# One Trainium2 core, a two-block transformer kernel: the first norm's scales by GpSimd's power operation

## The chip, the cores and the metric

The kernel runs on one core of one Trainium2 chip, as one launch. A core has five engines with queues of their own: TensorE (PE; its weight loads are listed apart as PEld), VectorE (DVE), ScalarE (ACT), GpSimd (POOL) and SyncE (SP), which here issues most DMA transfers. The metric is device time in microseconds (us) of the whole execution; the time of a kernel is the median of several runs.

## The reference, cut to what matters

A sequence of 512 rows of width 1024 goes through two transformer blocks in float32. Only the opening of the first block is touched by this change:

```python
h = x * rsqrt(mean(x * x, axis=-1) + 1e-6) * norm_mix      # rmsnorm, x is 512 x 1024
p = h @ w_in                                               # 1024 x 3872
# p feeds a retention mixer (rope from positions, chunks of 128)
# and an RWKV-7 mixer (token shift, decay and gate from low-rank products,
# a recurrence over time); then cross-attention over a memory of 256 rows,
# an MLP, and a second block with attention and a gated spatial mixer.
```

## The kernel before

Everything is held in float32, and a product that has to be exact is made as three reduced products: each operand is split into a high part (`wh`, or the first tile of a pair) and a low part (`wl`), and `mm3` multiplies high by high, high by low and low by high. The weights come as 189 units of 128x1024 in the order of use. For each unit SP issues one DMA into a `raw` buffer, ScalarE makes `wh` by a cast (line 291), and VectorE or GpSimd makes `wl` by a subtraction (line 292); the function is `pump(u, ahead, SC, E)`, and with `E` given that engine does the subtraction. `raw` has three buffers, so unit 3's transfer waits until unit 0 has been split.

`first()` is the opening. The rows of x are loaded as four blocks of 128 rows, `xb[0]` to `xb[3]`, by SP in the order block 0, block 1, the gain row `g` spread over 128 partitions, block 2, block 3, then units 0 and 1, constants, unit 2. Four helpers work on a block b: `square(b)` sums its squares on ScalarE; `chain(i)` makes the reciprocal roots of a pair of blocks on VectorE, by an integer guess and three Newton steps on 128x2 numbers (13 instructions with the scaling of the mean); `scale(b)` multiplies the block by its root and by the gain, in two halves of 512 columns; `turn(b)` transposes the scaled block on TensorE, four 128x128 tiles to a PSUM bank, and splits each bank into high and low, the high part by a cast on ScalarE and the low part by a subtraction on VectorE (`transp`, `psplit`). Blocks 0 and 1 are scaled on VectorE by one instruction that multiplies by root and gain together. For blocks 2 and 3 GpSimd multiplies x by the gain beforehand and ScalarE multiplies by the root.

After the turns, 48 matmuls of 256 columns make the first product `wa` (unit 0), first for rows 0 to 255 and then for rows 256 to 511; the PSUM tile `ps` is returned. Three pumps are in `first()`: unit 0 with its subtraction on GpSimd, unit 1 on VectorE, unit 2 on GpSimd.

`V`, `SC` and `G` in `first()` are the three engines wrapped by `Ordered`, which keeps the instructions that go through one wrapper in the order of the program; TensorE's wrapper `T` does so for the whole kernel. All other instructions are put in order, engine by engine, by a planner that simulates the program while it is built. The wrapper `G` is kept as `self.G`: `trig()` issues through it the argument reduction for sine and cosine of the retention's rope, 54 GpSimd instructions, nearly all on 128x128 numbers (the first one is the cast to `posf`), so these come behind all that `first()` puts on GpSimd. The two `Sin` activations (line 687) are on ScalarE. In the trace all that goes through a wrapper carries line 220.

After `first()`, `main()` runs one product after another (`tile_t`, 24 matmuls of 512 columns for a unit) and spawns side work (`lora`, `key`, `value`, `recept`) that uses the same engines between the products; its parts in the trace are lines 1412 to 1492.

Of the kernel before, what the change touches and what calls it, by code (L numbers as in the profile page):

```python
# [12 lines left out]
AF = mybir.ActivationFunctionType  # L13
ALU = mybir.AluOpType
# [4 lines left out]
NB = 4  # L19
D = 1024  # L20
KT = 8
# [207 lines left out]
class Kern:  # L229
# [74 lines left out]
    def mm3(self, ps, a, b, first, last):  # L304
        (ah, al), (bh, bl) = a, b
        mm = self.T.matmul
        mm(ps, ah, bh, start=first, stop=False)
        mm(ps, ah, bl, start=False, stop=False)
        mm(ps, al, bh, start=False, stop=last)
# [128 lines left out]
    def first(self):  # L438

        nc, A = self.nc, self.A  # L440
        self.zb = self.mp.tile([P, 128], mybir.dt.bfloat16, name="zb")
        nc.gpsimd.memset(self.zb, 0.0)
        xa, xc = self.slab(4, [P, 2, 1024]), self.slab(5, [P, 2, 1024])
        xb = [xa[:, 0], xa[:, 1], xc[:, 0], xc[:, 1]]
        ya, yc = self.slab(8, [P, 2, 1024]), self.slab(9, [P, 2, 1024])
        xg = [ya[:, 0], ya[:, 1], yc[:, 0], yc[:, 1]]
        ident = self.cp.tile([P, P], F32, name="ident")
        nc.scalar.dma_start(ident, A["cst"][:, 0:P])
        self.ident = ident
        load = lambda b: nc.sync.dma_start(xb[b], A["x"][b * 128:b * 128 + 128])  # L450
        load(0)
        load(1)
        g = self.gain("norm_mix", 6)
        load(2)
        load(3)
        self.prefetch(0)
        self.prefetch(1)
        derived = self.consts()
        self.prefetch(2)
        hh, h1 = self.act4((0, 1, 2, 3))  # L460

        V, SC, G = Ordered(self.tc, nc.vector), Ordered(self.tc, nc.scalar), Ordered(self.tc, nc.gpsimd)
        v = [self.small(2) for _ in range(2)]
        rs = {}
        junk = self.slab(10, [P, 1024])

        def square(b):
            SC.activation(junk, xb[b], AF.Square, accum_out=v[b // 2][:, b % 2:b % 2 + 1])

        def chain(i):  # L470
            V.tensor_scalar(v[i], v[i], 1.0 / D, 1e-6, op0=ALU.mult, op1=ALU.add)
            r = self.rsqrt(v[i], 2, V=V)
            rs[2 * i], rs[2 * i + 1] = r[:, 0:1], r[:, 1:2]

        def scale(b):
            for h in range(2):
                c = slice(h * 512, h * 512 + 512)
                if b < 2:
                    V.scalar_tensor_tensor(xg[b][:, c], xb[b][:, c], rs[b], g[:, c], op0=ALU.mult, op1=ALU.mult)
                else:  # L480
                    SC.activation(xg[b][:, c], xg[b][:, c], AF.Copy, scale=rs[b])

        turn = lambda b: self.transp(xg[b], b, hh, V, SC, ("tp", "ch")[b % 2])
        for b in range(NB):
            square(b)
        for b in (2, 3):
            G.tensor_tensor(xg[b], xb[b], g, op=ALU.mult)
        chain(0)
        scale(0)
        scale(1)  # L490
        chain(1)
        turn(0)
        self.pump(0, 0, SC, G)
        turn(1)
        scale(2)
        scale(3)
        turn(2)
        turn(3)
        h, l = self.spl.pop(0)
        self.u = 1  # L500
        ps = self.psum("mm")
        for off in (0, 256):
            for k in range(KT):
                ah, al = h1[k]
                self.mm3(ps[:, off:off + 256], (h[:, k * 128:k * 128 + 128], l[:, k * 128:k * 128 + 128]),
                         (ah[:, off:off + 256], al[:, off:off + 256]), k == 0, k == KT - 1)
        derived(V)
        self.pump(1, 0, SC, V)
        self.pump(2, 0, SC, G)
        self.G = G  # L510
        return h1, ps
# [1191 lines left out]
```

## Time and profile before

| | us |
|---|---|
| median of 3 runs | 1331.93 |
| lowest and highest of them | 1331.39, 1334.37 |
| the profiled execution, its own time | 1330.39 |
| its span in the trace | 1328.6 |
| TensorE busy in the span | 1257.8 (95%) |
| VectorE, GpSimd, ScalarE busy | 699.8, 536.7, 507.7 |

The span runs from the first to the last instruction of the trace; the profiled execution's own time is 1.79 us more. A view of the trace gives the start of an instruction in us from the start of the span, then its length; in brackets stand the time that its engine sat idle before it and what ended that wait. A line with "x4" holds four instructions, and its length then reaches from the start of the first to the end of the last. TensorE's clock is given as the granted share, where 1.00 is 2.4 GHz and 0.50 is 1.2 GHz.

### The profile page before, as it was taken

Reading aid. Unit: us, or ns where it says so; the run is one execution under the profiler, and the core shown is the slowest. Engines: PE = TensorE matmul, PEld = TensorE weight load, DVE = VectorE, ACT = ScalarE, POOL = GpSimd, SP = SyncE. Lnnn points to the kernel's source line nnn. Section 1 sums busy time; section 2 is a strip of 40 time slices with the busy share of each in tenths; the row PEclk is TensorE's granted clock in tenths of the full one; section 3 lists DMA queues with packets and bytes.
Section 4 is the critical chain, followed back from the end, with each engine's and each line's share of the span. In section 5 each row is a group of like instructions: output and inputs, shape, how many; then the busy total and the mean of one; then the engine's idle time right before and its main releaser. Section 6 shows DMA issues by size and latency. Waiting matters only on the chain.

```text
span 1328.6 us, 18213 instructions
## 1 busy us (share of the span) xinstructions
PE 1257.8 (95%) x6988; PEld 1043.1 (79%) x6988; DVE 699.8 (53%) x1465; ACT 507.7 (38%) x899; POOL 536.7 (40%) x544
## 2 busy tenths in 40 slices
PE   4999799998997989998999999999999999999997
PEld 4667577887895888888888888888887888788886
DVE  5667424456495275546333333332779946665355
ACT  5434323333344234433433322332534435554332
POOL 4924545135666553246311111110214563222474
PEclk9989899899999999999999999999999999999999
DMA  5223313211234422313333233333332232122321
GB/s 188 76 62 83 76 53 72 74 56 41 80 113 143 141 64 80 95 49 111 111 95 96 95 95 96 96 100 100 101 114 80 80 111 64 48 64 64 111 80 64
DMA packets 52376, 117.06 MB, mean 88 GB/s; under 512 B 23072, under 2 KB 23712, under 8 KB 52288
## 3 DMA queue, kind: packets, MB, share of 16 engines
q1 hardware_dynamic: 52112, 115.82, 28.6%
q8 instruction: 55, 0.90, 0.3%
q14 instruction: 33, 0.27, 0.1%
q0 software_dynamic: 32, 0.00, 0.0%
q10 hardware_dynamic: 144, 0.07, 0.0%
HBM read 112.46 MB, written 3.41 MB: 87 GB/s over the span
## 4 chain that ended last, share of the span: by engine, by line
PE 78%; POOL 7%; DVE 7%; issue 3%; ACT 2%; DMA 2%; SPq 0%; DVEq 0%; ACTq 0%; POOLq 0%
PE mm L220 64%; PE ch L220 7%; PE tp L220 4%; POOL s L220 3%; PE cs L220 3%; POOL o L1581 1%; DVE sm L362 1%; POOL s L1583 1%; DVE s L873 1%; DVE sm L358 1%; DMA s<-x 1%; DMA s<-dm 1%; POOL wl L220 0%; ACT t L1056 0%; ACT wh L291 0%
## 5 line engine op out<-in xcount | busy, mean ns | idle before, releaser
L220 PE MATMUL mm<-s,wh 128*128 128x512 f32 (+1 forms) x1424 | 422.5, 378 | 0.0
L220 PE MATMUL mm<-wh,s 128*128 128x512 f32 (+1 forms) x1264 | 364.1, 364 | 7.8 <-DVE s L873 7.8
L220 PEld LDWEIGHTS mm<-s,wh 128*128 128x128 f32 x1424 | 259.1, 191 | 53.2 <-issue 9.7
L220 PEld LDWEIGHTS mm<-wh,s 128*128 128x128 f32 x1264 | 231.2, 192 | 47.2 <-DVE s L873 9.6
L220 PE MATMUL mm<-s,wl 128*128 128x512 f32 (+1 forms) x704 | 263.5, 374 | 0.0
L291 ACT CAST wh<-raw 128x1024 fp32r<-128x1024 f32 x151 | 158.6, 1051 | 250.2 <-PE mm L220 220.2
L292 POOL TENSOR_TENSOR wl<-raw,wh 128x1024 fp32r<-128x1024 f32 x75 | 180.5, 2408 | 156.7 <-ACT wh L291 140.5
L220 PE MATMUL mm<-wl,s 128*128 128x512 f32 (+1 forms) x632 | 227.0, 359 | 2.0 <-POOL wl L292 1.7
L292 DVE TENSOR_TENSOR wl<-raw,wh 128x1024 fp32r<-128x1024 f32 x76 | 95.3, 1253 | 120.9 <-ACT wh L291 120.6
L220 PEld LDWEIGHTS mm<-s,wl 128*128 128x128 f32 x704 | 134.2, 191 | 21.3
L220 PEld LDWEIGHTS mm<-wl,s 128*128 128x128 f32 x632 | 121.9, 193 | 19.1 <-POOL wl L292 2.1
L1074 POOL TENSOR_TENSOR t<-t 128x512 f32<-128x512 f32 x32 | 50.0, 1563 | 214.8 <-ACT t L1073 214.8
L220 PE MATMUL mm<-s,whx 128*128 128x512 f32 (+1 forms) x336 | 100.2, 378 | 0.0
L220 PE MATMUL mm<-whx,s 128*128 128x512 f32 (+1 forms) x272 | 86.5, 377 | 0.6 <-DVE s L873 0.6
L347 DVE TENSOR_TENSOR s<-t,s 128x512 fp32r<-128x512 f32 x44 | 38.6, 877 | 69.9 <-ACT s L346 69.9
L292 POOL TENSOR_TENSOR wlx<-raw,whx 128x1024 fp32r<-128x1024 f32 x18 | 43.7, 2426 | 75.0 <-ACT whx L291 75.0
L220 PEld LDWEIGHTS mm<-s,whx 128*128 128x128 f32 x336 | 62.2, 194 | 10.6 <-DVE s L873 0.4
L220 PE MATMUL ch<-s,s 128*64 128x64 f32 (+3 forms) x504 | 65.2, 274 | 2.5 <-DVE s L873 1.8
L938 DVE TENSOR_TENSOR s<-mm,s 128x256 f32<-128x256 f32 x96 | 35.7, 419 | 58.7 <-PE mm L220 58.5
L291 ACT CAST whx<-raw 128x1024 fp32r<-128x1024 f32 x35 | 36.8, 1052 | 70.6 <-PE mm L220 54.4
L220 PE MATMUL mm<-s,wlx 128*128 128x512 f32 (+1 forms) x168 | 63.2, 376 | 0.0
L220 PEld LDWEIGHTS ch<-s,s 128*64 128x64 f32 (+2 forms) x504 | 47.0, 154 | 16.5 <-DVE s L873 3.7
(268 smaller groups left out, 1703.6 us busy)
## 6 DMA issues: line engine op xcount, KB each, us to landing
raw<-wst SPq DMA_DIRECT2D x189, 512.0 KB, 3.6
s<-x SPq DMA_DIRECT2D x8, 512.0 KB, 5.6
s<-rows SPq DMA_DIRECT2D x7, 512.0 KB, 4.0
out<-t SPq DMA_DIRECT2D x8, 256.0 KB, 2.3
t<-mem SPq DMA_DIRECT2D x2, 512.0 KB, 3.9
dm<-s SPq DMA_DIRECT2D x10, 64.0 KB, 2.0
s<-dm SPq DMA_DIRECT2D x2, 256.0 KB, 4.3
s<-dm SPq DMA_DIRECT2D x8, 64.0 KB, 2.5
```

The lines of the kernel that those rows point to most:

```text
L220: r = getattr(self.eng, name)(*a, **k)
L291: (SC or nc.scalar).copy(h, r)
L292: (E or (nc.gpsimd if self.lowpart(self.nspl) else nc.vector)).tensor_tensor(l, r, h.bitcast(F32), op=ALU.subtract)
L347: self.nc.vector.tensor_tensor(dst[1], src, dst[0].bitcast(F32), op=ALU.subtract)
L358: V.scalar_tensor_tensor(t, y, h, y, op0=ALU.mult, op1=ALU.mult)
L362: V.scalar_tensor_tensor(y, t, 1.5, y, op0=ALU.add, op1=ALU.mult)
L873: (V or self.nc.vector).tensor_tensor(dst[1], ps, dst[0].bitcast(F32), op=ALU.subtract)
L938: self.nc.vector.tensor_tensor(xs, ps[:, c], xs, op=ALU.add)
L1074: nc.gpsimd.tensor_tensor(q, r, r, op=ALU.mult)
L1581: G.tensor_tensor(tv, w[:, 0:k, s:s + 1].broadcast_to([P, k, n]), m[:, s:s + 1, s + 1:32].broadcast_to([P, k, n]), op=ALU.mult)
L1583: G.tensor_tensor(w[:, 0:k, s + 1:32], w[:, 0:k, s + 1:32], tv, op=ALU.add)
```

## The change

The reciprocal roots of the first norm are no longer made by Newton steps on VectorE for pairs of blocks. For each block by itself VectorE adds the epsilon to the mean, and GpSimd raises it to the power -0.5 with one 128x1 instruction, whose exponent comes from a small tile `mh` that GpSimd fills at the start. All four blocks are scaled on VectorE by the instruction that multiplies by root and gain together, so GpSimd's two multiplications by the gain and ScalarE's four multiplications by the root are gone. Unit 0's low part is made on VectorE instead of GpSimd. The order is written anew: `square(3)` comes behind the casts of `turn(0)`, `scale(2)` and `scale(3)` come between the turns, and the product of rows 0 to 255 is cut in two, with k from 0 to 3 issued between `turn(2)` and `turn(3)` and k from 4 to 7 behind `turn(3)`.

```diff
--- before.py
+++ after.py
@@ -460,50 +460,50 @@
         hh, h1 = self.act4((0, 1, 2, 3))
 
         V, SC, G = Ordered(self.tc, nc.vector), Ordered(self.tc, nc.scalar), Ordered(self.tc, nc.gpsimd)
-        v = [self.small(2) for _ in range(2)]
-        rs = {}
+        v = self.small(4)
+        rs, mh = self.small(4), self.small(4)
+        G.memset(mh, -0.5)
         junk = self.slab(10, [P, 1024])
 
         def square(b):
-            SC.activation(junk, xb[b], AF.Square, accum_out=v[b // 2][:, b % 2:b % 2 + 1])
-
-        def chain(i):
-            V.tensor_scalar(v[i], v[i], 1.0 / D, 1e-6, op0=ALU.mult, op1=ALU.add)
-            r = self.rsqrt(v[i], 2, V=V)
-            rs[2 * i], rs[2 * i + 1] = r[:, 0:1], r[:, 1:2]
+            SC.activation(junk, xb[b], AF.Square, accum_out=v[:, b:b + 1])
 
         def scale(b):
+
+            V.tensor_scalar(v[:, b:b + 1], v[:, b:b + 1], 1.0 / D, 1e-6, op0=ALU.mult, op1=ALU.add)
+            G.tensor_tensor(rs[:, b:b + 1], v[:, b:b + 1], mh[:, b:b + 1], op=ALU.pow)
             for h in range(2):
                 c = slice(h * 512, h * 512 + 512)
-                if b < 2:
-                    V.scalar_tensor_tensor(xg[b][:, c], xb[b][:, c], rs[b], g[:, c], op0=ALU.mult, op1=ALU.mult)
-                else:
-                    SC.activation(xg[b][:, c], xg[b][:, c], AF.Copy, scale=rs[b])
+                V.scalar_tensor_tensor(xg[b][:, c], xb[b][:, c], rs[:, b:b + 1], g[:, c], op0=ALU.mult, op1=ALU.mult)
 
         turn = lambda b: self.transp(xg[b], b, hh, V, SC, ("tp", "ch")[b % 2])
-        for b in range(NB):
-            square(b)
-        for b in (2, 3):
-            G.tensor_tensor(xg[b], xb[b], g, op=ALU.mult)
-        chain(0)
-        scale(0)
-        scale(1)
-        chain(1)
-        turn(0)
-        self.pump(0, 0, SC, G)
-        turn(1)
-        scale(2)
-        scale(3)
-        turn(2)
-        turn(3)
-        h, l = self.spl.pop(0)
-        self.u = 1
-        ps = self.psum("mm")
-        for off in (0, 256):
-            for k in range(KT):
+
+        def product(off, ks):
+            h, l = wa
+            for k in ks:
                 ah, al = h1[k]
                 self.mm3(ps[:, off:off + 256], (h[:, k * 128:k * 128 + 128], l[:, k * 128:k * 128 + 128]),
                          (ah[:, off:off + 256], al[:, off:off + 256]), k == 0, k == KT - 1)
+
+        square(0)
+        square(1)
+        square(2)
+        scale(0)
+        scale(1)
+        turn(0)
+        square(3)
+        scale(2)
+        turn(1)
+        self.pump(0, 0, SC, V)
+        wa = self.spl.pop(0)
+        self.u = 1
+        scale(3)
+        turn(2)
+        ps = self.psum("mm")
+        product(0, range(4))
+        turn(3)
+        product(0, range(4, 8))
+        product(256, range(8))
         derived(V)
         self.pump(1, 0, SC, V)
         self.pump(2, 0, SC, G)
```

## Rows read from the trace of the kernel before

**Rows 1.** The page: busy us of the engines; shares of the chain.

```profile
PE 1257.8 (95%) x6988; PEld 1043.1 (79%) x6988; DVE 699.8 (53%) x1465; ACT 507.7 (38%) x899; POOL 536.7 (40%) x544
...
PE 78%; POOL 7%; DVE 7%; issue 3%; ACT 2%; DMA 2%; SPq 0%; DVEq 0%; ACTq 0%; POOLq 0%
```

**Rows 2.** The chain that ended last, 0 to 90: start, us, what.

```profile
28.09 2.50 POOL wl L220
...
72.62 0.31 ACT sin L687
...
76.78 1.77 PE tp L220 x2
```

**Rows 3.** VectorE in order of time, 0 to 42.

```profile
7.25 0.65 DVE L220 TENSOR_SCALAR sm<-sm 128x2 f32<-128x2 f32 x4 [7.25 <-ACT s L220]
...
9.62 6.93 DVE L220 SCALAR_TENSOR_TENSOR s<-s,sm,s 128x512 f32<-128x512 f32 x4
...
10.29 5.60 DVE L220 SCALAR_TENSOR_TENSOR s<-s,sm,s 128x512 f32<-128x512 f32 x2
...
16.47 2.79 DVE L220 TENSOR_SCALAR sm<-sm 128x2 f32<-128x2 f32 x4
...
20.86 1.28 DVE L220 TENSOR_TENSOR s<-tp,s 128x512 fp32r<-128x512 f32 x2
...
27.10 1.23 DVE L220 TENSOR_TENSOR wl<-raw,wh 128x1024 fp32r<-128x1024 f32 x1
```

**Rows 4.** ScalarE in order of time, 0 to 42.

```profile
1.18 1.28 ACT L220 ACT_TABLE_LOAD   x1 [1.18 <-PEq L1696]
...
5.64 0.19 ACT L220 ACTIVATION_READ_ACCUMULATOR s<-s 128x1 f32 x1
...
6.06 1.06 ACT L220 ACTIVATE s<-s 128x1024 f32<-128x1024 f32 x1 [0.23 <-DMA s<-x]
...
9.69 1.06 ACT L220 ACTIVATE s<-s 128x1024 f32<-128x1024 f32 x1 [2.48 <-DMA s<-x]
...
25.53 0.59 ACT L220 CAST s<-ch 128x512 fp32r<-128x512 f32 x1 [0.27 <-PE ch L220]
...
26.01 2.00 ACT L220 CAST wh<-raw 128x1024 fp32r<-128x1024 f32 x2
```

**Rows 5.** GpSimd in order of time, 0 to 42.

```profile
9.76 5.58 POOL L220 TENSOR_TENSOR s<-s,s 128x1024 f32<-128x1024 f32 x2 [6.00 <-DMA s<-x]
...
15.95 2.81 POOL L220 TENSOR_TENSOR wl<-raw,wh 128x1024 fp32r<-128x1024 f32 x1 [0.61 <-ACT wh L220]
...
30.53 0.19 POOL L220 CAST posf<-posi 128x4 f32<-128x4 int32 x1
...
35.26 0.45 POOL L220 TENSOR_TENSOR s<-s 128x128 f32<-128x128 f32 x1
```

**Rows 6.** TensorE in order of time, pieces of 0 to 90.

```profile
21.82 1.97 PE L220 MATMUL tp<-ident,s 128*128 128x128 f32 x8 [3.91 <-ACT s L220]
...
25.15 0.78 PE L220 MATMUL mm<-s,wh 128*128 128x256 f32 x2
...
31.32 0.63 PE L220 MATMUL mm<-s,wh 128*128 128x512 f32 x2
...
76.78 1.77 PE L220 MATMUL tp<-t,cst 2*128 2x512 f32 x2 [2.55 <-ACT t L1448]
...
82.06 1.91 PE L220 MATMUL ch<-ident,t 128*128 128x128 f32 x8
```

**Rows 7.** SP's DMA queue, 0 to 10: the issue that waited for the gain row.

```profile
8.39 0.33 SPq L533 DMA_DIRECT2D s<-lora  x1
```

**Rows 8.** Waits of SP's queue, 0 to 10: us in total, times, longest.

```profile
SPq L533 <- DMA s<-rows: 2.0, 1, 2.0
```

**Rows 9.** Windows: length, busy PE, PEld, DVE, ACT, POOL, granted clock, DMA.

```profile
78.00:80.00 2.00, 2.00 (x5) 1.23 (x5) 1.41 (x3) 0.60 (x2) 0.31 (x2) 0.50 0.00 0
...
82.00:84.00 2.00, 2.00 (x10) 1.94 (x9) 1.29 (x3) 0.58 (x1) 0.00 (x0) 0.51 0.00 0
```

## The prediction

> **What bounds the kernel now.** I read the page first: TensorE is busy for 1257.8 us, 95% of the span, and 78% of the chain that ended last is its own work [rows 1]. So what happens before TensorE's steady run moves the end one for one, unless a second chain stands beside it. I followed the chain of waits through the first 90 us and then each engine in order of time. The chain does not join TensorE at its first product. From 28.09 us it is GpSimd's: unit 2's low part, then the sine reduction without a gap until ScalarE's `Sin` at 72.62, then the `tanh` and copy work queued behind it, and only at 76.78 TensorE, which had waited 2.55 us for it [rows 2, 6]. The reduction cannot begin before unit 2's low part (its first cast, to `posf`, is at 30.53 [rows 5]), and that starts 0.08 us after ScalarE's two casts of units 1 and 2, from 26.01 to 28.01 [rows 4]. These casts follow the last cast of `turn(3)`, which begins at 25.53. So the date that counts is that cast, and the price of the whole change is how much earlier it comes. TensorE's own date beside it is the first matmul of unit 1, at 31.32 [rows 6].
>
> Why is that cast so late? A multiplication of `scale(0)` and `scale(1)` gives way to the next after 0.67 us when nothing is in the way (9.62 to 10.29), but the second and third take 2.8 us each (5.60 for both), next to GpSimd's two multiplications in 5.58 us; the four take 6.93 [rows 3, 5]. The first of the small instructions of `chain(1)` is stretched the same way next to GpSimd's subtraction at 15.95, so that four of them take 2.79 us, and the other nine run to 20.9. Only then ScalarE can scale blocks 2 and 3.
>
> **The change part by part.** *Removed.* GpSimd's two multiplications and its subtraction, 5.58 + 2.81 us, and with them the stretching: four multiplications on VectorE fall from 6.93 to some 2.8 us. Both Newton chains go, 26 small instructions, of which `chain(1)` held VectorE from 16.47 to 20.9 us. ScalarE's four multiplications, which waited for `chain(1)`, go too.
>
> *Added on VectorE's path.* Four more multiplications of 0.67 us = 2.7, unit 0's subtraction 1.23 (as unit 1's at 27.10 [rows 3]), and four round trips to GpSimd. A round trip is the small instruction, 0.16 (four of them in 0.65 [rows 3]), a hand-over of 0.08 each way (as ScalarE to GpSimd above) and the power itself. VectorE is in order, so it stands still meanwhile: `scale(1)` waits behind it, and behind `scale(2)` the subtractions of `turn(1)`. No row shows a power. From below the nearest row is a GpSimd cast of 128x4, 0.19 us; from above a whole pass over 1024 columns, 2.81 us [rows 5]. A power of one number per partition is nearer to the small ones; I take the 0.45 us of a 128x128 product, which is to say that one power costs as much as 128 multiplications. A round trip is then 0.16 + 0.16 + 0.45 = 0.77 us.
>
> The Trainium skill (GPSIMD Reference, 2.1 Instruction dispatch) says that the first call of a freshly loaded kernel pays about 6 us for loading code; no row here shows this, and by it the sum would be an estimated 1332.4 us, 3.8 later.
>
> *The new order, step by step.* `square(0)` ends at 5.83 [rows 4], so the first power is ready at some 6.6. The gain row stands in the way: SP's issue that waited 2.0 us for it goes out at 8.39 [rows 7, 8]. I take 8.4 for the first multiplication, against 9.62 before. VectorE then:
> - `scale(0)`, 2 x 0.67: to 9.76
> - `scale(1)`, 0.77 + 1.34: to 11.87
> - two subtractions of `turn(0)`, pitch 0.6 (two in 1.28 [rows 3]): to 13.07. Their casts come behind `square(2)`, whose block lands at 9.6 and which ends at 10.9 [rows 4]; they end at 12.0, in time.
> - `scale(2)`: to 15.18
> - subtractions of `turn(1)`: to 16.4. ScalarE does `square(3)` from 12.0 to 13.3 and these casts to 14.4, in time; then unit 0's cast to 15.5.
> - unit 0's subtraction: to 17.6
> - `scale(3)`: to 19.7.
>
> TensorE has `turn(2)` done by then, and two of the twelve matmuls of the first part of the product; the third needs unit 0's low part, so ten remain at 17.6. Their price depends on the clock. The 48 matmuls of this product run from 25.15 to 31.32, 0.13 us each, but the first two take 0.78 together. The transposes tell why: eight take 1.97 us at 21.82 and 1.91 at 82.06, inside a window granted 0.51 [rows 6, 9]. So up to some 26 us TensorE is at the lower level, whatever the share printed there, and the clock rose with TensorE at work without a gap since 21.82. I cost the ten at twice 0.13: to 20.2. `scale(3)` ends first, so `turn(3)` starts at 20.2, its eight transposes end at 22.2, and its last cast starts there instead of at 25.53. From that cast to the end of unit 2's cast it was 28.01 - 25.53 = 2.48 us, so it is now at 24.7: 3.3 us earlier.
>
> The remaining 36 matmuls of the product take 0.13 each at the higher level, 4.7 us, or 6.2 if the first twelve are still slow: unit 1 starts at 26.9 to 28.4, earlier by 2.9 to 4.4. Its low part is there by 25 (cast to 23.8, subtraction 1.23). TensorE's date moves about as far as GpSimd's or farther, and TensorE waits later, at 76.78, for GpSimd's branch, so GpSimd's 3.3 us is what the chain gets. GpSimd's four powers lie in a stretch where it now has nothing else, and `mh` is filled at the start. SP's queue is unchanged: raw 3 leaves once unit 0 is split, at 17.6 instead of 18.8. The weight DMAs and everything behind 77 us hang on these dates alone and move along.
>
> Against the profiled execution's own 1330.39 the sum is 1327.1. That execution lies 1.54 below the median of 1331.93, so I forecast **1328.6 us** as a median. A measurement of this kernel tells about 0.2%, 2.7 us, from no change, so this is just beyond it.
>
> **The bounds.** The power enters twice (`scale(1)` and `scale(2)`) as long as the ten matmuls end after `scale(3)`, that is up to 1.55 us; beyond that three times. At 0.19 us the gain is 3.3 + 2 x 0.26 = 3.8. At 2.81 it is 3.3 - 2 x 1.1 - 3 x 1.26 = -2.7, and `scale(0)`'s own power, out at 8.9, adds 0.5: 3.2 us slower. If the ten run at 0.13 they end at 18.9; `turn(3)` then starts behind the first half of `scale(3)`, at 19.1, and ends at 21.1, or, if its transposes are faster too, half of them behind the second half, at some 20.4: 1.1 to 1.8 more gain, 1326.8 to 1327.5.
>
> **The rivals.**
> 1. *Part of the gain is eaten inside the opening.* Either a power of 0.75 to 1.9 us (gain 2.7 down to 0), or a wait of `scale(0)` for `square(2)`, since the four sums are now columns of one tile and `square(2)` comes first in the program: the first multiplication then starts at 10.9 + 0.77 = 11.7 instead of 8.4, and the gain is gone. For such a wait speaks nothing but the order; against it that `square(0)` is through at 5.83 while `square(1)` still waits, to 6.06, for the other half of the same slab to land [rows 4]. Or a first power that loads code: it has 8.4 - 6.1 = 2.3 us of cover, and at the price of ScalarE's table load, 1.28 us [rows 4], it would be hidden; a load of 5.6 us would eat all. Time 1329 to 1332; chance 0.27.
> 2. *It ends slower: the power itself.* Its place is `scale(1)` to `scale(3)` on VectorE, its price three times its length. At 1.9 us the gain is gone, and from 2.7 the kernel is slower by over 0.2%; at 2.81 it gives 1335.1. For it: a power is many steps per number in software, and no row bounds it. Against: one number per partition, and 128 of the simplest cost 0.45. Chance 0.15, with what little slower the next rival may bring.
> 3. *The join at 72 to 77 us changes.* The planner sets the order anew, and the `Sin` pair with a table load on either side may fall elsewhere in ScalarE's queue. Behind the copy of line 1448, TensorE loses its 2.55 us wait, and with it perhaps the stretch at the lower clock that follows (78 to 84 [rows 9], of which half is lost). The gain is then 3.3 + 2.55 to 3.3 + 2.55 + 3: 1323 to 1326. Nothing in the order of the program asks for it. Chance 0.13.
>
> **How the numbers follow.** The forecast has 0.45 and its own range is 1326.8 to 1329.5, the rivals 0.27, 0.15 and 0.13. Leaving out the better half of rival 3 and most of rival 2, the range is 1324.5 to 1333.5. Faster by over 0.2% are the forecast, where its range does not reach past 1329.3, rival 3 and the best of rival 1: 0.58. Within 0.2%: most of rival 1, the forecast's worst end and the near part of rival 2: 0.28. Slower: 0.14.
>
> **What the profile will show.** Right: first multiplication at 8.4; eight multiplications of 0.7 us none of which is stretched; powers below 0.6 us; last cast of `turn(3)` near 22; unit 2's low part near 24.8 and `Sin` near 69.3, unit 1's first matmul at 27 to 28.5. Wrong: gaps of over 1 us on VectorE ahead of `scale(1)`, `scale(2)` and `scale(3)`; `turn(3)` waiting for the matmuls longer than to 20.2; or a `Sin` that does not move with unit 2's low part, which would mean that GpSimd's order has changed.

## The result, and the profile after

The median of five runs was 1322.73 us (1317.90 to 1324.92), against 1333.15 of before in the same session; ratio 0.9928, with a 95% interval of 0.9904 to 0.9953. A second measurement (below) gave 1323.80 against 1330.53, ratio 0.9940 (0.9919 to 0.9961). So the change gains some 7 to 10 us, two to three times the 3.3 us of the forecast, and the time lies under the range. The profiled execution took 1322.73 us, its span is 1321.0. One execution of run 18 below took 4181.76 us; its ratio leaves it out, its median (1325.87, without it 1325.51) does not.

The page, busy us of the engines and shares of the chain, against [rows 1]:

```profile
PE 1252.4 (95%) x6988; PEld 1038.9 (79%) x6988; DVE 693.2 (52%) x1448; ACT 507.4 (38%) x897; POOL 531.3 (40%) x546
...
PE 75%; POOL 9%; DVE 8%; issue 3%; ACT 3%; DMA 2%; SPq 0%; DVEq 0%; ACTq 0%; POOLq 0%
```

The opening. VectorE in order of time, 0 to 30, against [rows 3]:

```profile
5.96 0.15 DVE L220 TENSOR_SCALAR sm<-sm 128x1 f32<-128x1 f32 x1 [5.96 <-ACT s L220]
9.28 1.41 DVE L220 SCALAR_TENSOR_TENSOR s<-s,sm,s 128x512 f32<-128x512 f32 x2 [3.17 <-DMA s<-rows]
10.61 0.15 DVE L220 TENSOR_SCALAR sm<-sm 128x1 f32<-128x1 f32 x1
11.43 1.42 DVE L220 SCALAR_TENSOR_TENSOR s<-s,sm,s 128x512 f32<-128x512 f32 x2 [0.67 <-POOL sm L220]
...
17.30 1.22 DVE L220 TENSOR_TENSOR wl<-raw,wh 128x1024 fp32r<-128x1024 f32 x1
...
19.24 1.41 DVE L220 SCALAR_TENSOR_TENSOR s<-s,sm,s 128x512 f32<-128x512 f32 x2 [0.66 <-POOL sm L220]
```

GpSimd, the same stretch, against [rows 5]:

```profile
6.20 0.57 POOL L220 TENSOR_TENSOR sm<-sm,sm 128x1 f32<-128x1 f32 x1 [2.38 <-DVE sm L220]
10.84 0.56 POOL L220 TENSOR_TENSOR sm<-sm,sm 128x1 f32<-128x1 f32 x1 [4.07 <-DVE sm L220]
...
25.37 2.49 POOL L220 TENSOR_TENSOR wl<-raw,wh 128x1024 fp32r<-128x1024 f32 x1 [6.17 <-ACT wh L220]
27.81 0.19 POOL L220 CAST posf<-posi 128x4 f32<-128x4 int32 x1
```

ScalarE, the opening and the join, against [rows 2, 4]:

```profile
22.82 0.59 ACT L220 CAST s<-ch 128x512 fp32r<-128x512 f32 x1 [0.27 <-PE ch L220]
23.30 2.00 ACT L220 CAST wh<-raw 128x1024 fp32r<-128x1024 f32 x2
...
69.46 0.31 ACT L687 ACTIVATE sin<-s 128x128 f32<-128x128 f32 x1 [0.54 <-POOL s L220]
69.79 1.28 ACT L1419 ACT_TABLE_LOAD   x1
71.08 0.69 ACT L1419 ACTIVATE kt<-tp,hv 128x512 f32<-128x512 f32 x1
71.79 1.28 ACT L687 ACT_TABLE_LOAD   x1
73.08 0.31 ACT L687 ACTIVATE cos<-s 128x128 f32<-128x128 f32 x1
73.30 0.56 ACT L1448 COPY t<-ch 2x512 f32<-2x512 f32 x1
```

TensorE, pieces of 13 to 80, against [rows 6]:

```profile
18.57 0.58 PE L220 MATMUL mm<-s,wl 128*128 128x256 f32 x1 [1.35 <-DVE sm L220]
...
20.87 1.91 PE L220 MATMUL ch<-ident,s 128*128 128x128 f32 x8
...
27.61 0.63 PE L220 MATMUL mm<-s,wh 128*128 128x512 f32 x2
...
73.91 2.07 PE L220 MATMUL tp<-t,cst 2*128 2x512 f32 x2 [3.86 <-ACT t L1448]
```

and one window behind the join (length, busy PE, PEld, DVE, ACT, POOL, granted clock, DMA), against [rows 9]:

```profile
76.00:78.00 2.00, 2.00 (x5) 1.61 (x6) 1.95 (x4) 0.32 (x1) 0.74 (x2) 0.50 0.00 0
```

The reader is to see three things. No multiplication is stretched any more: every pair takes 1.41 or 1.42 us. VectorE stands 0.66 or 0.67 us for each power after the first. And the branch of the forecast has moved as a whole: unit 2's low part from 28.09 to 25.37, `Sin` from 72.62 to 69.46, TensorE's pass at the join from 76.78 to 73.91, 2.9 us earlier.

But 2.9 is not 7. The dates of TensorE's matmuls (numbered from 0 in order of start) show where the rest appears: number 300, behind the join, starts at 85.07 instead of 88.89; number 1400 at 238.28 instead of 246.61; the last at 1312.44 instead of 1320.38. So in this pair of traces some 4 us more are gained between 85 and 247 us, and nothing behind. In the second pair (runs 3 and 4 below) the gain is 2.1 us at matmul 300, 4.5 at matmul 1400 and 8.3 at the last, so there 3.8 us are gained behind matmul 1400. Between matmuls 300 and 1400 the clock differs. Windows of 130 to 250: length, busy PE, granted clock, DMA; first of before, then of after:

```profile
130.00:150.00 20.00, 16.14 (x74) 0.91 0.19 60
150.00:170.00 20.00, 14.81 (x130) 0.74 0.43 92
170.00:190.00 20.00, 19.75 (x180) 0.91 0.23 61
190.00:210.00 20.00, 20.00 (x148) 1.00 0.19 53
210.00:230.00 20.00, 17.39 (x178) 0.93 0.44 93
230.00:250.00 20.00, 20.00 (x206) 0.73 0.16 51
```

```profile
130.00:150.00 20.00, 16.63 (x90) 0.91 0.20 55
150.00:170.00 20.00, 14.39 (x174) 0.74 0.37 71
170.00:190.00 20.00, 20.00 (x145) 1.00 0.28 81
190.00:210.00 20.00, 19.82 (x155) 1.00 0.12 34
210.00:230.00 20.00, 16.68 (x182) 0.83 0.46 93
230.00:250.00 20.00, 20.00 (x226) 1.00 0.37 123
```

One minus the clock, times 20 us, summed: 15.6 us lost before, 10.4 after. The difference, 5.2, is close to the 4.5 us (8.33 less 3.82) that the dates of matmuls 300 and 1400 show.

### The profile page after: what moved, and what is told of

Read it like the earlier page. It is cut to its first block, busy times and chain, and to the rows that moved or that the text cites. A ratio compares the mean times of both kernels' runs of the same rounds, so it can differ in the third digit from the quotient of the medians.

```text
span 1321.0 us, 18197 instructions
## 1 busy us (share of the span) xinstructions
PE 1252.4 (95%) x6988; PEld 1038.9 (79%) x6988; DVE 693.2 (52%) x1448; ACT 507.4 (38%) x897; POOL 531.3 (40%) x546
## 4 chain that ended last, share of the span: by engine, by line
PE 75%; POOL 9%; DVE 8%; issue 3%; ACT 3%; DMA 2%; SPq 0%; DVEq 0%; ACTq 0%; POOLq 0%
PE mm L220 63%; PE ch L220 6%; PE tp L220 4%; POOL s L220 3%; PE cs L220 3%; POOL o L1581 2%; POOL s L1583 1%; POOL t L1583 1%; DVE sm L362 1%; DVE s L873 1%; DVE sm L358 1%; DMA s<-rows 1%; DMA raw<-wst 1%; DMA s<-dm 0%; ACT wh L291 0%
## 5 line engine op out<-in xcount | busy, mean ns | idle before, releaser
L292 POOL TENSOR_TENSOR wl<-raw,wh 128x1024 fp32r<-128x1024 f32 x75 | 180.5, 2409 | 157.6 <-ACT wh L291 144.7
L220 PEld LDWEIGHTS mm<-s,whx 128*128 128x128 f32 x336 | 62.5, 194 | 10.4 <-issue 0.2
```

The costliest lines, as they stand in the source:

```text
L220: r = getattr(self.eng, name)(*a, **k)
L292: (E or (nc.gpsimd if self.lowpart(self.nspl) else nc.vector)).tensor_tensor(l, r, h.bitcast(F32), op=ALU.subtract)
```

## The experiments

The question is what sets the gain: the date of GpSimd's branch (the forecast), TensorE's own opening, the order that the planner gives to what follows, or the clock. Each kernel is compared with the kernel before on the same chip.

**The parts of the opening.** Run 1 keeps the new order and makes the roots by Newton steps on VectorE for each block; run 2 repeats block 3's multiplications ahead of `turn(3)`; runs 3 and 4 are the kernels before and after once more.

```diff
 # run 1, in scale(b)
-            G.tensor_tensor(rs[:, b:b + 1], v[:, b:b + 1], mh[:, b:b + 1], op=ALU.pow)
+            r = self.rsqrt(v[:, b:b + 1], 1, V=V)
 # run 2, behind scale(3) and turn(2)
+        for h in (0, 1, 0, 1):
+            c = slice(h * 512, h * 512 + 512)
+            V.scalar_tensor_tensor(xg[3][:, c], xb[3][:, c], rs[:, 3:4], g[:, c], op0=ALU.mult, op1=ALU.mult)
```

> The changed kernel with one thing undone: the root of each block is made by ten small Newton instructions on VectorE instead of GpSimd's power. The planner's order behind the opening is that of the changed kernel on ScalarE, and on GpSimd but for neighbours that change places. Ten small instructions at about 0.2 us are 2.0 us against a round trip of some 0.8 us, so VectorE's path to the last turn grows by 1.2 us three times, of which the wait for the matmuls hides some: the last cast of the last turn should come 2.5 to 3.6 us later than in the changed kernel (22.8), unit 1's first matmul at 30.1 to 31.2 instead of 27.6. Theory 'order' (4.5 of the 7.6 to 9.6 us gained come from the planner's other order behind 60 us): the total is that of the changed kernel plus 2.5 to 3.6, so 1325 to 1327, still 5 to 7 below the kernel before. Theory 'clock' (those 4.5 are where the stretches of low clock happen to fall in an execution): the total falls anywhere between that and 1331, and one execution differs from the next by as much.

> The changed kernel with four more multiplications of the last block on VectorE (the same values written again), 4 x 0.67 = 2.7 us ahead of the last turn. The last cast comes 2.5 us later than in the changed kernel, unit 2's low part at 27.9. The planner puts the pair of Sin activations together again, as in the kernel before, and leaves the second inversion as in the changed kernel, up to neighbours. Theory 'order': the total is that of the changed kernel plus 2.5, some 1325, and the join behind the Sin costs what it cost before (TensorE's wait 2.5 us). Theory 'clock': anywhere from 1325 to 1331. Theory 'opening alone' (a microsecond at the opening is a microsecond at the end): plus 2.5 exactly, by either.

> The kernel before, unchanged, for a second trace. Theory 'order': it again waits some 2.2 us for the second inversion's transfer at 226 us and loses there what it lost in the first trace; its times lie within 1331 to 1335. Theory 'clock': the low stretches behind 140 us (four in the first trace, two of them second ones after a first) fall elsewhere, and the time at TensorE's 1400th matmul differs from 246.6 by 2 us or more.

> The changed kernel, unchanged, for a second trace and more times. Theory 'order': TensorE's 1400th matmul is again near 238.3, and the times lie within 1318 to 1325. Theory 'clock': the number and place of low stretches behind 140 us differ from the first trace (two), and the 1400th matmul moves by 2 us or more with them. Either way the opening should repeat within 0.5 us, but for the landing of the gain row (9.15 here, 8.4 in the kernel before).

Measured: run 1 1331.06 us, ratio 1.0006 (0.9988 to 1.0024); run 2 1329.65, 0.9984 (0.9966 to 1.0002); run 3 1330.34, 0.9993 (0.9972 to 1.0014); run 4 1323.80, 0.9940 (0.9919 to 0.9961). In run 1 a chain takes 0.59 + 1.31 us where a power with its way there and back takes 0.15 + 0.67. Here are VectorE's first chain, unit 2's low part and `Sin` of run 1:

```profile
6.08 0.59 DVE L220 TENSOR_SCALAR sm<-sm 128x1 f32<-128x1 f32 x4 [6.08 <-ACT s L220]
6.71 1.31 DVE L220 SCALAR_TENSOR_TENSOR sm<-sm,sm 128x1 f32<-128x1 f32 x6
...
26.98 2.57 POOL L220 TENSOR_TENSOR wl<-raw,wh 128x1024 fp32r<-128x1024 f32 x1 [23.22 <-ACT wh L220]
...
72.45 0.31 ACT L685 ACTIVATE sin<-s 128x128 f32<-128x128 f32 x1 [2.18 <-POOL s L220]
```

TensorE's first product of run 1 was 2.8 us earlier than before's (matmul 72 at 27.51 for 30.36), but `Sin` only 0.17, and nothing was gained. Unit 2's low part did start 1.1 us earlier; GpSimd took 42.95 us from the cast to `posf` to `Sin`, for 42.08, so the length of the branch is itself not fixed to the microsecond. Run 1's order on TensorE and ScalarE is that of the kernel after, and on GpSimd nearly so. So neither TensorE's own opening nor the planner's order carries the gain; what is left is the date of the branch. Run 2 fits this: `Sin` comes earlier, at 70.52, but three table loads between it and the copy take this back, and its matmul 300 starts at 89.18. Runs 3 and 4 show how far two executions of one kernel differ: matmul 1400 starts at 244.10 in run 3 for 246.61, and at 239.61 in run 4 for 238.28.

**The branch by itself.** Runs 7 and 8 move only unit 2's low part from GpSimd to VectorE, in the kernel before and in the kernel after. Runs 5 and 6 were to take the copy that TensorE waits for off ScalarE, but caught that of the other pair of heads (`key(p, ...)` is called for each pair); run 16 took the right one.

```diff
 # runs 7 and 8, in first()
-        self.pump(2, 0, SC, G)
+        self.pump(2, 0, SC, V)
 # runs 5 and 6 (p == 0) and 16 (p == 1), in key()
-        SC.copy(rts[0:2], rt[0:2].rearrange("p a b -> p (a b)"))
+        (V.tensor_copy if p == 1 else SC.copy)(rts[0:2], rt[0:2].rearrange("p a b -> p (a b)"))
```

> The kernel before, but unit 2's low part is made on VectorE, so that GpSimd's sine reduction starts 2.5 us earlier and nothing of the first norm is touched. If the branch through the sine sets the join, as the prediction had it, Sin comes near 70.1, the join and all behind it 2.3 to 2.5 us earlier: 1328. If the gain of the kernel after comes from TensorE's own opening instead (unit 1 at 27.6 for 31.3), this gives nothing: 1330.5. If an earlier join is worth twice its size, as it looked in the kernel after, 1325.

> The same edit on the kernel after. By the branch: Sin near 67, TensorE's wait of 3.9 us falls to 1.5, a further 2.4 us: 1321. By TensorE's own opening: as after, 1323.5. By an earlier join worth twice its size: 1318 to 1319.

> The kernel before, but the first copy of line 1448, behind which TensorE waits at 76.78, is made on VectorE, so it no longer stands behind the Sin pair and its table loads in ScalarE's queue. Theory 'TensorE's own date': what counts behind the join is when TensorE gets past it; the wait of 2.55 us goes and with it the low clock that follows (3.4 us lost there): 1325 to 1328 against 1330.5. Rival 'branch': the exp of pt, and with it the inversion whose result TensorE waits for 5 us near 146, still stands behind Sin; TensorE only waits longer there, and the time stays within 1 us of 1330.5.

> The same edit on the kernel after, where TensorE waits 3.9 us for that copy. 'TensorE's own date': 3.9 us faster than after, and by the low clock up to 3 more, 1317 to 1320. 'Branch': as after, 1323 to 1324, the wait near 140 us longer by what the join lost.

> The kernel before, with the copy that TensorE waits 2.55 us for at 76.78 made on VectorE. 'TensorE's own date': TensorE passes at some 74.3, 2.5 us and the low clock behind it are gained, 1325 to 1327. 'Branch': the exp of pt and what hangs on it still come behind Sin at 72.6, TensorE waits 2.5 us longer for the first inversion near 146, and the time stays at 1330.5, less 1 to 2 for the order of the second inversion that the planner changes with it, as in run 5.

Measured: run 7 1324.26 against 1331.82, ratio 0.9956 (0.9934 to 0.9979); run 8 1320.97, 0.9924 (0.9902 to 0.9946), the lowest median of all kernels here; run 5 1328.75, 0.9981 (0.9965 to 0.9997); run 6 1323.27, 0.9939 (0.9919 to 0.9959); run 16 1332.07 against 1331.15, 1.0002 (0.9980 to 1.0024). Run 7, in order of time: `Sin` on ScalarE, TensorE at the join:

```profile
65.05 0.31 ACT L687 ACTIVATE sin<-s 128x128 f32<-128x128 f32 x1 [1.75 <-POOL s L220]
...
75.72 1.12 PE L220 MATMUL tp<-t,cst 2*128 2x512 f32 x2
```

and its window 60 to 90 (busy of PE, PEld, DVE, ACT and POOL, granted clock, DMA):

```profile
60.00:90.00 30.00, 27.12 (x130) 19.25 (x129) 21.84 (x39) 14.83 (x21) 8.77 (x14) 1.00 0.24 72
```

Without a stroke of work on the norm, the kernel before gains 7.6 us by its medians (some 5.9 by the ratio, whose interval overlaps that of run 4): most of what the whole change gave. `Sin` comes 7.6 us earlier, not 2.3: the sine reduction no longer stands behind the cast of unit 2 at all (its first cast is at 20.49 instead of 30.53). TensorE's wait at the join is gone, and with it the stretch at the lower clock (1.00 in the window, 0.50 in [rows 9]). But TensorE passes the join only 1.1 us earlier than in the kernel before (75.72 for 76.78), because now its own work sets the date; the 4.3 us by which matmul 300 is earlier are for the most part the clock. In run 8, too, TensorE passes without a wait, at 72.93. Its median is the 1321 that the branch was to give, though by way of no wait at all, where 1.5 us of it were to be left.

Runs 5 and 6 say how loosely the end follows. Run 5 leaves the join as it was (TensorE passes at 77.16 after 2.54 us of waiting), and its median is 3.1 us lower. In run 6 the planner put the two `Sin` side by side again; TensorE passes at 71.59, 2.3 us earlier than in the kernel after, and the median is not clearly lower than that kernel's.

Run 16 did not do what it was meant to. TensorE, then ScalarE's exp, then the copy on VectorE:

```profile
78.14 2.04 PE L220 MATMUL tp<-t,cst 2*128 2x512 f32 x2 [3.91 <-ACT pt L1420]
...
77.46 0.63 ACT L1420 ACTIVATE pt<-t 128x512 f32<-128x512 f32 x1 [1.18 <-DVE t L1415]
...
77.34 0.65 DVE L1448 COPY t<-ch 2x512 f32<-2x512 f32 x1
```

The copy is not out of the way: VectorE makes it at 77.34, 1.2 us later than ScalarE did (76.17), behind the scan of line 1415, which waits for a `tanh` behind `Sin`. It ends at 77.99, and TensorE passes 1.4 us later than in the kernel before. The view names the exp of `pt`, which ends 0.10 us after the copy; but in run 7 the same matmul ran at 75.72, before that exp began at 76.40, so it does not need it. So both engines' queues stand behind `Sin` here, and what a copy free of the branch would bring remains untested.

**The product in one piece.** Run 11 takes one part of the change back: the product of rows 0 to 255 stands whole behind `turn(3)`.

```diff
-        ps = self.psum("mm")
-        product(0, range(4))
         turn(3)
-        product(0, range(4, 8))
+        ps = self.psum("mm")
+        product(0, range(8))
```

> The kernel after, but the product of rows 0 to 255 whole behind turn(3), as the kernel before had it. turn(3) no longer waits for the ten matmuls from 18.95 to 20.87: its casts, unit 2's cast and GpSimd's branch come 1.5 us earlier (unit 2's low part at 23.9, Sin at 68), TensorE's unit 1 about 1 us later (28.6). By the branch, the join comes 1.5 us earlier and the time is 1322 or, with the clock, 1320; if TensorE's own opening sets the end, it is 1 us later, 1324.5.

Measured: 1324.83 against 1330.04, ratio 0.9971 (0.9948 to 0.9994). The branch's dates came as expected, and unit 1 began 0.4 us later than in the kernel after, at 28.00 (ScalarE, then TensorE of run 11):

```profile
67.81 0.31 ACT L686 ACTIVATE sin<-s 128x128 f32<-128x128 f32 x1 [4.67 <-POOL s L220]
...
73.09 1.12 PE L220 MATMUL tp<-t,cst 2*128 2x512 f32 x2 [2.83 <-ACT t L1447]
```

Unit 2's low part starts at 23.95 and matmul 300 at 83.57, 1.5 us earlier than in the kernel after. Yet the median is not lower; it is the 1324.5 that the expectation gave for TensorE's own opening, though TensorE's date behind the join, 1.5 us earlier, speaks against that theory. The profiled execution was the fastest of the twelve, 1317.97 us, so trace and median are not of one kind here. An earlier join is not handed on one for one.

**The clock.** Products by zero (128x512, 0.22 us each) were put into TensorE's waits, to see what the lower clock behind a wait costs. The first two attempts missed: the fillers of runs 9, 10 and 12 fell between 538 and 574 us, those of runs 13 to 15 began at 423.81 (run 14), behind three of the four waits, and the first of them itself waited the 1.40 us of the fourth. They measure something else: 22 or 26 more matmuls, 4.8 or 5.6 us, in the steady run. Runs 17 and 18 filled the join.

```diff
 # runs 13 to 15, in quad(), which makes a product from four units: 8, 6 and 7 in its first call, 5 in its second;
 # runs 9, 10, 12: the same matmul under another count, 7, 5, 6 and 4 in a later call
+                for f in range(F):
+                    self.T.matmul(ps[b], self.zb, self.zb.unsqueeze(1).broadcast_to([P, 4, 128]), start=q == 0 and f == 0, stop=False)
 # and the first real matmul of such a sum adds to them instead of starting it
 # run 17 (9 of them; 14 in run 18), in key(), ahead of the matmul that waits for the copy
+        for _ in range(9 if p == 1 else 0):
+            self.T.matmul(bc, self.zb, self.zb.unsqueeze(1).broadcast_to([P, 4, 128]), start=True, stop=True)
```

> The kernel before, with 22 products by zero issued on TensorE into the waits for the four heads near 390 to 425 us (they add zero to the sums; nothing else changes its order). Theory 'clock': a good part of what the kernel after gains beyond the join (some 4 us) is that in most executions of the kernel before 6.8 to 17 us around these waits run at the lower clock, and in the kernel after 3.4. Filled, the clock stays up there: 2 to 5 us faster than before, 1326 to 1329 against 1331, and fewer executions above 1331. Rival 'dates': the clock there is the same in both and the gain is of dates alone; the fillers give nothing or cost 1 us.

> The same fillers in the kernel after, whose two traces show one stretch of 3.4 us there. By 'clock' 1 to 2 us faster than after, 1321.5 to 1323, so the distance between the two kernels shrinks from 7 to 4 to 6 us; by 'dates' as after, 1323.5, and the distance stays 7.

> The kernel after with unit 2's low part on VectorE and the fillers in the waits for the heads. If the two add up: 1320.97 less 1 to 2 us, 1319 to 1320. If the clock takes back what the fillers give (as it did with the 3 us earlier join of the run with the copy on VectorE): 1321 to 1322.

> The kernel before with 26 products by zero (0.22 us each) in TensorE's four waits at 390 to 425 us, 8, 6, 7 and 5; the order of every other engine is unchanged. 'Clock': the low stretches behind these waits go (3.4 to 17 us of them in the traces, half of which is lost): 2 to 4 us faster than before, 1327 to 1329. 'Dates': no change, or 1 us slower where a wait was shorter than its fillers.

> The same in the kernel after, whose traces have 3.4 us of low clock there. 'Clock': 1 to 2 us faster than 1323.5, and the distance to run 13 is 4 to 5 us instead of 7. 'Dates': 1323.5 or 1 us slower, distance 7.

> The kernel after with unit 2's low part on VectorE and the same fillers. 'Clock': 2 to 3 us below the 1321.0 of run 8, 1318 to 1319. 'Dates': 1321.

> The kernel before, with 9 products by zero (some 0.22 us each) issued on TensorE into its wait at 74.2 to 76.8, all other orders unchanged. 'Clock': the stretch at half the clock behind the join (77 to 84) goes, TensorE is 3.4 us earlier by 90 us and, as the time behind is bound by TensorE, 2 to 4 us faster at the end: 1327 to 1329. 'Dates': the branch comes no earlier, the first inversion takes back what TensorE gained: 1331.

> The same in the kernel after, 14 products into its wait at 70.0 to 73.9 (the planner shifts some GpSimd products of the second inversion with it). 'Clock': 2 to 4 us faster than 1323.5, 1319.5 to 1321.5. 'Dates': 1323.5.

Measured, 4.8 us more: run 9 (before) 1335.92 against 1330.04, ratio 1.0059 (1.0033 to 1.0085); run 10 (after) 1325.31, 0.9972 (0.9953 to 0.9991); run 12 (run 8's kernel) 1325.80, 0.9984 (0.9957 to 1.0011). With 5.6 us more: run 13 1338.32 against 1331.15, 1.0067 (1.0042 to 1.0091); run 14 1330.20, 1.0005 (0.9987 to 1.0023); run 15 1327.44, 0.9983 (0.9964 to 1.0003). So 4.8 us cost 5.9, 1.5 to 2.6 and 4.8; 5.6 cost 7.2, 6.4 to 7.5 and 6.5 (the second and third of each against medians of other sessions). They don't test the clock at 390 to 425 us, which stays open.

Run 17, TensorE at the join in order of time:

```profile
75.61 2.10 PE L220 MATMUL tp<-zb 128*128 128x512 bf16 x9 [1.52 <-ACT t L1412]
77.64 1.12 PE L220 MATMUL tp<-t,cst 2*128 2x512 f32 x2
```

and two windows behind it:

```profile
78.00:80.00 2.00, 2.00 (x8) 1.09 (x7) 1.20 (x3) 0.46 (x1) 0.19 (x1) 1.00 0.00 0
...
82.00:84.00 2.00, 2.00 (x10) 1.68 (x9) 2.00 (x4) 1.91 (x3) 0.00 (x0) 1.00 0.00 0
```

The lower clock of [rows 9] is gone from this stretch. The fillers ended 0.9 us past the old wait (the real matmul is at 77.64 for 76.78), and still matmul 300 starts at 86.52, for 88.89 and 87.61 in the two traces of before. The time is 1330.94 against 1330.20, ratio 1.0005 (0.9985 to 1.0025): nothing at the end. Run 18 (after) took 1325.87, 0.9967 (0.9947 to 0.9987), no gain over the kernel after; but it is no test, for its fourteen fillers did not keep the clock up. Its window behind the join:

```profile
76.00:78.00 2.00, 2.00 (x6) 1.42 (x6) 1.97 (x3) 0.11 (x1) 1.77 (x2) 0.50 0.00 0
```

So in the kernel before, by run 17 alone, the end does not hang on the fall of the clock at the join. Its trace is 5.0 us ahead of the mean of before at matmul 1400 and loses that behind it: from there to the last matmul it needs 1081.8 us, for 1073.8 and 1077.8.

**All of them together.** The start of `Sin` and of matmul 300 (fillers not counted) in one trace each, what is gained at matmul 300 against the mean of the two traces of before (88.25), and the gain of the median over that of before in the same session, us:

```
kernel                         Sin            matmul 300     gained there   gained in the median
before, run 3                  72.62, 72.91   88.89, 87.61   -0.6, 0.6       -, 0.2
after, run 4                   69.46, 69.18   85.07, 85.55    3.2, 2.7      10.4, 6.7
1  Newton steps                72.45          88.07           0.2           -0.5
2  later turn(3)               70.52          89.18          -0.9            0.9
5  before, other copy          73.00          87.65           0.6            3.1
6  after, other copy           68.49          82.11           6.1            8.6
7  before, unit 2 on VectorE   65.05          84.61           3.6            7.6
8  after, unit 2 on VectorE    60.83          81.81           6.4           10.9
11 after, product whole        67.81          83.57           4.7            5.2
16 before, join's copy         72.62          89.67          -1.4           -0.9
17 before, filled join         72.47          86.52           1.7           -0.7
18 after, filled join          69.25          84.18           4.1            4.3
```

A straight line through the 13 pairs has a slope of 1.4 and misses them by 2.3 us (root mean square). The date behind the join and the end go together, but the time behind it has a spread of its own that is as large as most gains; and each date is from one execution, each median from five to twelve.

## Why the prediction was wrong

**The opening was right.** The first multiplication was put at 8.4; it came at 9.28 here and at 8.34 in run 4 (the gain row's landing moves between executions). A round trip was put at 0.77 and took 0.82; the power, the one unknown price, at 0.45 and took 0.55 to 0.57. The ten matmuls were to end at 20.2 and ended at 20.87; the last cast of `turn(3)` came at 22.82 (21.86 in run 4) for 22.2, unit 2's cast ended at 25.30 (24.35) for 24.7. So the 3.3 us were 2.7 in one trace and 3.7 in the other. Unit 1's first matmul, put at 26.9 to 28.4, started at 27.61.

**The first two rivals did not happen.** No wait for `square(2)`: the first small instruction is at 5.96. The power is far from the 1.9 us at which the gain would be gone. The Trainium skill (GPSIMD Engine Reference, 2.1 Instruction dispatch) has the first call of a freshly loaded kernel pay some 6 us; the first power took 0.57 us, the second 0.56, so nothing of this kind shows in this trace.

**The join was right, for the reason given.** `Sin` was put near 69.3 and started at 69.46; TensorE still waits for the copy behind it, and passes 2.9 us earlier. Runs 7 and 8 show that GpSimd's branch is what it waits for: with unit 2's low part off GpSimd the wait is gone. Rival 3 came nearest to the times that were measured (1323 to 1326, against 1322.73 and 1323.80), but not in its way: `Sin` did not get behind the copy, TensorE's wait there grew from 2.55 to 3.86 us, and the stretch at the lower clock stayed behind it (0.50 from 76 to 78 us). What the planner did change, with a second table load between `sin` and the copy, came to 0.3 us (4.45 from `sin` to the join, for 4.16).

**The step that failed** is the last of the sum: "everything behind 77 us hang on these dates alone and move along". The two traces of after are 2.9 us ahead of the two of before at matmul 300, and 8.1 us at the last. From matmul 300 to 1400 the two of before need 157.7 and 156.5 us, the two of after 153.2 and 154.1: 3.5 us between the means; the work is the same, and the windows show that the clock makes the difference. The other 1.7 us lie behind matmul 1400, and there one execution of before is alone: run 3 needs 1077.8 us to the last matmul, the other trace of before 1073.8, the two of after 1074.2 and 1073.9. [rows 9] had the price of one such stretch, half of its length; the prediction spent it on the join alone and took all later ones to be the same in both kernels. Its base was a median of three executions, 1331.93, and carried a spread too: the median of before lay between 1330.04 and 1333.15 us in the six sessions here.

**What stays open** is why they differ. Runs 9 and 13, and 10 and 14, had their fillers far behind matmul 1400 and the orders of before and after ahead of it, so they give two more traces of each kernel (TensorE from 90 to 250 us: length, busy, granted clock, DMA; runs 9, 13, 10, 14):

```profile
90.00:250.00 160.00, 146.90 (x1171) 0.94 0.30 76
90.00:250.00 160.00, 147.67 (x1130) 0.90 0.28 70
...
90.00:250.00 160.00, 146.06 (x1177) 0.94 0.30 78
90.00:250.00 160.00, 148.49 (x1173) 0.93 0.31 79
```

With them the gain at matmul 300 is 3.3 us (means of four, 88.49 and 85.20), which is what the forecast gave for the branch. From matmul 300 to 1400 runs 9 and 13 need 153.7 and 157.6 us, runs 10 and 14 153.7 and 153.8, so the four of after lie together and the four of before reach from there to 4 us more; the means differ by 2.7. Over all twenty traces this time follows the granted clock from 90 to 250 us: 157.6 and 157.7 at 0.90, 154.9 to 156.5 at 0.91, 153.6 to 154.9 at 0.93, 153.2 to 153.8 at 0.94, 150.5 at 0.95.

What sets the clock there is not known. It is not the planner's new order: run 17, with before's order everywhere, took 153.8 us for the same matmuls, run 1, with after's order on TensorE and ScalarE, 155.9, and runs 5 and 16, both with the same new order of the second inversion, 153.6 and 156.4. Nor does the clock at the join settle it (run 17). Which waits are followed by the lower clock differs between executions: the 30 runs of the kernel before in one session lie between 1323.1 and 1334.1 us, the ten of the kernel after in two sessions between 1317.9 and 1324.9. The Trainium skill (TensorE: Matmul & The Clock Gate, What's actually happening) says that the number of matmuls at the lower clock varies from run to run of one kernel, and says it of the start of a kernel. Behind later waits it varies here as well: 0.90 and 0.91 of full clock from 90 to 250 us in the first two traces of before, 0.94 and 0.90 in runs 9 and 13. More than the join's gain came out at the end with the change and with runs 7 and 8, not with runs 11 and 17. No run fixed the clock between 85 and 250 us, so the 2.7 us there, and what run 3 lost behind matmul 1400, are placed but not explained.

## What to carry to other kernels

Follow the chain to the place where it joins the bound engine, and ask first what feeds the branch: one subtraction moved to another engine brought most of what the rewritten norm brought, because the branch had been queued behind it. Moving the instruction that a wait names to another engine (the copy, in run 16) brings nothing when that engine's queue stands behind the same branch; look at its new date before you read the time. Where a gain is smaller than what one execution differs from the next, predict the date and add a spread: here 1.4 us at the end for 1 us at the join, give or take 2.3.

## What the runs showed of the hardware

- GpSimd's power of 128 numbers took 0.55 to 0.57 us, the first as the later ones, and 0.66 to 0.67 us as VectorE sees it: less than half of a Newton chain of ten small instructions on VectorE (1.9 us).
- Two multiplications of 128x512 on VectorE take 1.41 us when GpSimd does not multiply beside them, while the second and third of the old kernel, beside GpSimd's, took 5.60 [rows 3].
- Nine products by zero in a wait kept TensorE's granted clock at 1.00 from 78 to 84 us where it had been 0.50 (run 17); the end did not move. Fourteen in run 18 did not keep it: 0.50 from 76 to 78 us.
- 4.8 us of added work in TensorE's steady run changed the median by 1.5 to 5.9 us, in three kernels with the same program around it, two of them against medians of other sessions.
